# A hybrid DeltaNet and sparse-attention trunk on one core: the masks of the block inverse applied to its products, and background steps offered every 128 channels

## The chip, the core and the metric

The kernel runs on one core of one Trainium2 chip. The core has a matrix engine (TensorE, in the profile PE, its weight loads PEld) and three others that work on rows of elements: VectorE (DVE), ScalarE (ACT) and GpSimd (POOL). SyncE (SP) starts the loads of the weights. The engines run side by side, each through its own instructions in order, and wait for each other by semaphores. The metric is the time of one execution on the device, in microseconds (us).

## The reference, cut to what matters

One layer of gated DeltaNet, one of sparse attention, each followed by an MLP with squared ReLU, all with residual sums and RMS norms, for 256 tokens of width 2048. The part that the change touches is the DeltaNet layer's triangular system, for 32 value heads and chunks of 64 tokens:

```python
qkv, z, b, a = jnp.split(h @ w_in, [s1, s2, s3], axis=-1)
qkv = jax.nn.silu(_causal_conv(qkv, conv_w))        # four taps
l_mat = jnp.where(strict, jnp.einsum("nbhid,nbhjd->nbhij", kb, k) * decay, 0.0)
t_mat = lax.linalg.triangular_solve(eye + l_mat, eye, left_side=True, lower=True, unit_diagonal=True)
u = t_mat @ vb
w = t_mat @ (kb * jnp.exp(gc)[..., None])
...
o = rms_norm(o, out_norm) * jax.nn.silu(z)
```

## The kernel before, in words

All heavy products are of float32 numbers, each split into a high and a low part (the high part, whi, is a cast by ACT, the low part, wlo, a subtraction by DVE), and each product is three matmuls of such parts (`mm3`). The weights pass once: SP loads them in tiles of 1024 columns, and `Stream.get` (L144) splits the tile three places ahead before the matmuls of the present one are issued. So each weight tile brings one cast of 128x1024 on ACT and one subtraction of 128x1024 on DVE, always on time or TensorE waits.

Two helpers run over the weight tiles. `by_channel` (L359) takes two slices of 128 rows (k) per tile, and for each slice four blocks of 128 channels; a block is three matmuls of 256 columns, a slice 12, a tile 24. `by_token` (L377) has the tokens as the stationary side, and its matmuls are 512 columns wide, or 256 in the z projection.

Everything else in the program is background work: generators (`decays`, `delta`, `solved`, `transposed`, the attention's `attend` and others) that issue a piece, yield, and are resumed at a tick. `Background.tick` (L122) resumes a generator once its estimated time has come: the planner `Pace` (L36 to L70) keeps a clock for each engine by a formula of costs, and a step is due when the end of its chain plus 0.4 us is not after TensorE's clock. `yield True` also counts in the end of the last GpSimd operation. `ensure(key)` forces steps until an operand is there. So the order of the instructions on every engine is written at build time by this planner. In `by_channel` the tick stands behind each slice, that is after 12 matmuls.

The DeltaNet stage has 16 groups of two heads, each with eight weight tiles for q, k and v in `by_channel` and four for z in `by_token`. Behind the z tiles the group's two gates are made (zg: ACT's tanh, then a DVE product, twice). `delta` does the convolution (for each of four channels one ACT scaling and three DVE taps, y<-s,cw,y), the decays E (GpSimd), the products pk of keys and queries, and the factors la. Every second group, `solved` (L598) inverts the triangular factors of a pair of groups (eight pairs). It first copies the 32x32 diagonal blocks of la into Lc (16 small ACT copies), makes the inverse of the 2x2 diagonal blocks (Tct by two DVE operations, Tc by a transpose), and then goes through four levels (block sizes 2, 4, 8, 16). At each level: a product of 32 small matmuls in 32x32 tiles with a masked copy of Lc, a copy of it out of PSUM to Pm, a second product with Tct, a subtraction from Tc, a transpose to Tct. The four masked copies (Lm) are made by one GpSimd product of 128x1024 in the space of yv, which is why the profile calls them yv. Pm is Lc's own space, so the copies to Pm read Lc<-aux in the profile. Then come the 64-row and 128-row steps, the solutions, and four transposes of the output (aux<-wide,Tt) per chunk of heads, which the out-projection reads as h.

At the start of each MLP the residual sums of the last 512 columns (h<-acc,h on DVE, `chunk_done`) are transposed by a background generator (pk<-wide,h or aux<-wide,h), while `by_channel` has begun on the earlier columns. The engines' operations all pass through a helper, so every row of the profile says L81.

Of the kernel before, what the change touches and what calls it, by code (L numbers as in the profile page):

```python
# [11 lines left out]
OP = mybir.AluOpType  # L12
AX = mybir.AxisListType

P = 128
# [4 lines left out]
B = 32  # L20
LEVELS = (2, 4, 8, 16)
# [155 lines left out]
def tile_hybrid_trunk(ctx: ExitStack, tc: tile.TileContext, a: dict, out: bass.AP):  # L177
# [3 lines left out]
    act, dve, pool, pe = (pace.engine(n, e) for n, e in (("act", nc.scalar), ("dve", nc.vector), ("pool", nc.gpsimd), ("pe", nc.tensor)))  # L181
# [12 lines left out]
    bg = Background(pace)  # L194
    ws = Stream(pace, sync, act, dve, rawp, partp, 4, 4)

    def acc():
        return accp.tile([P, 512], F32, name="acc")
# [3 lines left out]
    def aux():  # L202
        if spare:
            spare.append(spare.pop(0))
            if spare[0]:
                return pkp.tile([P, 512], F32, name=spare[0])
        return auxp.tile([P, 512], F32, name="aux")
# [78 lines left out]
    fine = const.tile([P, 2 + len(LEVELS), B], F32, name="fine")  # L286
# [34 lines left out]
    def mm3(o, stat, mov, start, stop):  # L321
        (sh, sl), (mh, ml) = stat, mov
        pe.matmul(o, lhsT=sh, rhs=mh, start=start, stop=False, skip_group_check=True)
        pe.matmul(o, lhsT=sh, rhs=ml, start=False, stop=False, skip_group_check=True)
        pe.matmul(o, lhsT=sl, rhs=mh, start=False, stop=stop, skip_group_check=True)
# [19 lines left out]
    def ensure(key):  # L345
        while key not in ready:
            assert bg.step(), key
# [11 lines left out]
    def by_channel(n_items, part, key, n_ct=4, ahead=0):  # L359

        banks = [acc() for _ in range((n_ct + 1) // 2)]
        k0 = 0
        for _ in range(n_items):
            hi, lo = ws.get()
            n = hi.shape[1]
            for j in range(n):
                k = k0 + j
                ensure((key, min(k + ahead, n_items * n - 1)))
                for ct in range(n_ct):
                    s = slice(ct * P, ct * P + P)  # L370
                    mm3(banks[ct // 2][:, (ct % 2) * T:(ct % 2) * T + T], (hi[:, j, s], lo[:, j, s]), part(k),
                        k == 0 and ct % 2 == 0, False)
                bg.tick()
            k0 += n
        return banks

# [25 lines left out]
    with tc.tile_pool(name="first", bufs=1) as fp:  # L402
        xin = fp.tile([P, 2, D], F32, name="xin")
        rows = fp.tile([P, P], F32, name="rows")
# [8 lines left out]
        for name, src in (  # L413
# [3 lines left out]
            n = src.shape[0] // P  # L417
# [49 lines left out]
        bg.step()  # L467
        bg.step()
        first_banks = by_channel(8, x_part, "x0", ahead=3)
        bg.drain()  # L470

# [4 lines left out]
    with tc.tile_pool(name="delta", bufs=2, reuse_waits="tile") as dp:  # L476
# [43 lines left out]
        def delta(g, s, zg):  # L520
# [74 lines left out]
            if j == 1:  # L595
                yield from solved(p, *zip(*pairs[p]))

        def solved(p, la, r, rs, zg):  # L598

            H, U = range(4), [(i, b) for i in range(4) for b in range(2)]  # L600
            n_u = len(U)
            while p and ("o", 4 * p - 1) not in ready:
                yield
            rows = lambda q, n=1: slice(B * q, B * (q + n))
            flat = lambda x: x.rearrange("p u c -> p (u c)")
            one = lambda shape, name: dp.tile([P] + shape, F32, name=name, bufs=1)
            Lc, Tc, Tct = (one([n_u, B], n) for n in ("Lc", "Tc", "Tct"))
            Tt, yv = one([4, 2, P], "Tt"), one([4, 2, P], "yv")
            Pm, fold = Lc, yv.rearrange("p i b c -> p (i b c)")
            Lm = fold.rearrange("p (n u c) -> p n u c", n=len(LEVELS), u=n_u)  # L610
            pool.memset(Tt, 0.0)
            for j in range(2):
                for b in range(2):
                    for q in range(4):
# [3 lines left out]
            each = lambda x: x.unsqueeze(1).to_broadcast([P, n_u, B])  # L618
            n_l = len(LEVELS)
            dve.tensor_tensor(Tct, Lc, each(fine[:, 1]), op=OP.mult)  # L620
            dve.tensor_tensor(Tct, Tct, each(fine[:, 0]), op=OP.add)
            dve.transpose(flat(Tc), flat(Tct))
            pool.tensor_tensor(Lm, Lc.unsqueeze(1).to_broadcast([P, n_l, n_u, B]),
                               fine[:, 2:].unsqueeze(2).to_broadcast([P, n_l, n_u, B]), op=OP.mult)
            yield True
            small_bank = lambda w=B: aux()[:, 0:n_u * w].rearrange("p (u c) -> p u c", u=n_u)
            for n in range(n_l):
                t = small_bank()
                for u in range(n_u):
                    for q in range(4):  # L630
                        pe.matmul(t[rows(q), u], lhsT=Lm[rows(q), n, u], rhs=Tc[rows(q), u], start=True, stop=True)
                act.copy(Pm, t)
                yield
                t = small_bank()
                for u in range(n_u):
                    for q in range(4):
                        pe.matmul(t[rows(q), u], lhsT=Tct[rows(q), u], rhs=Pm[rows(q), u], start=True, stop=True)
                dve.tensor_tensor(Tc, Tc, t, op=OP.subtract)
                dve.transpose(flat(Tct), flat(Tc))
                yield  # L640
# [3 lines left out]
            t = small_bank()  # L644
# [11 lines left out]
            t = small_bank()  # L656
# [8 lines left out]
            t = small_bank(2 * B)  # L665
# [4 lines left out]
            t = small_bank(2 * B)  # L670
# [15 lines left out]
            t = aux()  # L686
# [10 lines left out]
            for j in range(2):  # L697
                t = aux().rearrange("p (i b d) -> p i b d", i=2, b=2)
# [27 lines left out]
            for j in range(2):  # L726
                t = aux()
# [8 lines left out]
        for g in range(DN_G):  # L736
            banks = first_banks if g == 0 else by_channel(8, x_part, "x0")
            if g > 1:
                ensure(("v", g - 2))
            s = dp.tile([P, 4, T], F32, name="s")  # L740
            for c in range(2):
                act.copy(s[:, 2 * c:2 * c + 2].rearrange("p n t -> p (n t)"), banks[c])
            if g == 0:
                bg.add(decays(by_channel(2, x_part, "x0", n_ct=1)[0]))
            zo = by_token(4, x_part, "x0", n_cols=256)
            if g > 4:
                ensure(("o", 2 * g - 9))
            zg = dp.tile([P, 2, T], F32, name="zg", bufs=5)
            for b in range(2):
                act.activation(zg[:, b], zo[b], AF.Tanh, scale=0.5)  # L750
                dve.scalar_tensor_tensor(zg[:, b], zg[:, b], 1.0, zo[b], op0=OP.add, op1=OP.mult)
            bg.add(delta(g, s, zg))
# [80 lines left out]
    with tc.tile_pool(name="dsa", bufs=1, reuse_waits="tile") as sp, ExitStack() as late:  # L833
# [165 lines left out]
        for c in range(4):  # L999
# [8 lines left out]
            for j in range(0, 4, 2):  # L1008
                if 4 * c + j >= 8:
                    ensure(("qa", 4 * c + j - 7))  # L1010
                t = acc()
                for i in range(2):
                    for k in range(2):
                        s = slice(k * P, k * P + P)
# [21 lines left out]
    for c in range(2):  # L1036
        s = slice(c * 1024, c * 1024 + 1024)
# [14 lines left out]
def _consts():  # L1052
    import numpy as np

    i, j = np.arange(P)[:, None], np.arange(P)[None, :]
    c = [np.eye(P), j >= i]
    i, j = i % B, j[:, :B]
    c += [i == j, -((i % 2 == 0) & (j == i + 1)).astype(np.float32)]
    for s in LEVELS:
        c.append((i // (2 * s) == j // (2 * s)) & (j % (2 * s) >= s) & (i % (2 * s) < s))  # L1060
    return np.concatenate([np.asarray(x, np.float32) for x in c], axis=1)


# [16 lines left out]
```

## Time and profile before

| what | value |
|---|---|
| median of 3 runs | 2609.01 us (2606.13 to 2609.33) |
| profiled execution | 2608.86 us |
| its span | 2607.1 us |
| mean granted clock of TensorE | 0.997 |
| TensorE (PE) busy | 98% of the span |
| DVE, ACT, POOL busy | 59%, 49%, 12% |

The span runs from the first to the last recorded instruction; the execution's own time has 1.8 us around it. A matmul's row gives its start and a modelled end: matmuls are pipelined, so the next one starts well before the row's end, and the time that a wait costs is best read from start to start. In the rows below "idle before" is the time in which the engine did nothing before the row, and the name behind the arrow is what it waited for. The DeltaNet stage lies between 135 and 790 us, the first MLP begins near 936 us.

### The profile page before, as it was taken

How to read it: one execution, taken by the hardware profiler on the slowest of the kernel's cores; microseconds unless marked ns; L12 is line 12 of the kernel's file. 1: busy time of each engine (PE TensorE's matmuls, PEld its weight loads, DVE VectorE, ACT ScalarE, POOL GpSimd, SP SyncE). 2: the span in 40 equal slices, each digit the busy share in tenths (PEclk: the TensorE clock that was granted, in tenths of full speed). 3: DMA queues.
4: the chain of work that ended last, by engine and by line, in shares of the span. 5: the costliest groups of instructions: out<-in, count | busy, mean ns of one | idle time of the engine just before them, and what ended most of it. 6: DMA issues, size and time to landing. Idle time of an engine off the chain costs nothing.

```text
span 2607.1 us, 52386 instructions
## 1 busy us (share of the span) xinstructions
PE 2559.3 (98%) x21795; PEld 2345.4 (90%) x21795; DVE 1534.1 (59%) x2164; ACT 1272.6 (49%) x1888; POOL 304.0 (12%) x514
## 2 busy tenths in 40 slices
PE   7999999999999999999999999999999999999997
PEld 7999999999978799988899988898899988999886
DVE  5867677768764555554455554676555544455544
ACT  5555555555554444443344444566444433444443
POOL 0434344434331000000000000000000000000000
PEclk9999999999999999999999999999999999999999
DMA  6655555555544566666666666644666666666664
GB/s 192 189 146 158 140 147 156 146 155 150 153 166 142 175 190 194 194 192 193 193 187 186 191 188 188 180 140 134 181 191 194 194 194 193 188 186 187 192 194 137
DMA packets 325389, 455.90 MB, mean 175 GB/s; under 512 B 18280, under 2 KB 159840, under 8 KB 324768
## 3 DMA queue, kind: packets, MB, share of 16 engines
q1 hardware_dynamic: 321888, 443.85, 56.9%
q10 hardware_dynamic: 2928, 7.37, 0.9%
q8 instruction: 170, 2.79, 0.4%
q0 software_dynamic: 336, 1.34, 0.2%
q14 instruction: 67, 0.55, 0.1%
HBM read 450.37 MB, written 2.13 MB: 174 GB/s over the span
## 4 chain that ended last, share of the span: by engine, by line
PE 90%; DVE 5%; ACT 2%; issue 1%; DMA 1%; POOL 0%; SPq 0%; ACTq 0%; DVEq 0%; POOLq 0%
PE acc L81 81%; PE aux L81 6%; PE pk L81 3%; DVE wlo L81 2%; ACT Lc L81 1%; DVE Tct L81 1%; DMA raw<-in_dn_w_in 1%; DVE y L81 1%; ACT whi L81 1%; DMA xin<-in_x 0%; DVE Tc L81 0%; ACT acc L81 0%; DVE p L81 0%; DVE h L81 0%; DVE Tt L81 0%
## 5 line engine op out<-in xcount | busy, mean ns | idle before, releaser
L81 DVE TENSOR_TENSOR wlo<-raw,whi 128x1024 fp32r<-128x1024 f32 x838 | 1027.2, 1233 | 869.7 <-ACT whi L81 860.4
L81 ACT CAST whi<-raw 128x1024 fp32r<-128x1024 f32 x838 | 874.1, 1048 | 865.4 <-PE acc L81 816.5
L81 PE MATMUL acc<-xhi,whi 128*128 128x256 f32 x3088 | 871.0, 282 | 0.3 <-ACT whi L81 0.3
L81 PE MATMUL acc<-xhi,wlo 128*128 128x256 f32 x3088 | 860.8, 279 | 1.2 <-DVE wlo L81 1.2
L81 PE MATMUL acc<-xlo,whi 128*128 128x256 f32 x3088 | 860.8, 279 | 0.0
L81 PE MATMUL acc<-whi,h 128*128 128x512 f32 x2688 | 847.2, 392 | 4.0 <-ACT acc L81 2.0
L81 PEld LDWEIGHTS acc<-whi,h 128*128 128x128 f32 x2688 | 504.8, 188 | 111.5 <-ACT acc L81 2.9
L81 PEld LDWEIGHTS acc<-xhi,wlo 128*128 128x128 f32 x3088 | 585.2, 190 | 1.7 <-DVE wlo L81 1.7
L81 PEld LDWEIGHTS acc<-xhi,whi 128*128 128x128 f32 x3088 | 581.4, 188 | 2.8 <-ACT whi L81 0.7
L81 PEld LDWEIGHTS acc<-xlo,whi 128*128 128x128 f32 x3088 | 581.8, 188 | 0.2
L81 PE MATMUL acc<-wlo,h 128*128 128x512 f32 x1344 | 524.6, 390 | 0.0
L81 PEld LDWEIGHTS acc<-wlo,h 128*128 128x128 f32 x1344 | 252.7, 188 | 50.1
L81 PE MATMUL acc<-whi,xhi 128*128 128x256 f32 (+2 forms) x576 | 171.4, 298 | 0.0
L81 PE MATMUL acc<-whi,xlo 128*128 128x256 f32 (+2 forms) x576 | 166.2, 288 | 0.0
L81 PE MATMUL acc<-wlo,xhi 128*128 128x256 f32 (+2 forms) x576 | 166.1, 288 | 0.0
L81 POOL TENSOR_SCALAR E<-R,tokc 128x128 f32<-128x128 f32 x96 | 104.5, 1103 | 144.9 <-DMA raw<-in_dn_w_in 81.2
L81 POOL DMA_DIRECT2D gain<-in_norm_final x1 | 0.7, 652 | 957.4 <-DVE nm L81 957.4
L81 PEld LDWEIGHTS acc<-whi,xhi 128*128 128x128 f32 x576 | 108.1, 188 | 2.6
L81 PEld LDWEIGHTS acc<-whi,xlo 128*128 128x128 f32 x576 | 108.2, 188 | 1.3
L81 PEld LDWEIGHTS acc<-wlo,xhi 128*128 128x128 f32 x576 | 108.1, 188 | 1.3
L81 DVE SCALAR_TENSOR_TENSOR y<-s,cw,y 128x255 f32<-128x255 f32 (+2 forms) x192 | 93.4, 487 | 13.3 <-ACT y L81 8.6
L81 POOL TENSOR_TENSOR h<-h,gain 128x512 f32<-128x512 f32 x8 | 10.1, 1282 | 777.4 <-ACT acc L81 777.4
(249 smaller groups left out, 1940.7 us busy)
## 6 DMA issues: line engine op xcount, KB each, us to landing
raw<-in_mlp_w_up SPq DMA_DIRECT2D x256, 512.0 KB, 4.3
raw<-in_mlp_w_down SPq DMA_DIRECT2D x256, 512.0 KB, 4.2
raw<-in_dn_w_in SPq DMA_DIRECT2D x66, 512.0 KB, 4.3
raw<-in_dn_w_in SPq DMA_DIRECT2D x256, 128.0 KB, 2.6
raw<-in_dn_w_in SPq DMA_DIRECT2D x128, 256.0 KB, 3.3
raw<-in_dn_w_out SPq DMA_DIRECT2D x64, 512.0 KB, 3.7
raw<-in_dsa_w_out SPq DMA_DIRECT2D x32, 512.0 KB, 4.0
raw<-in_dsa_w_uq SPq DMA_DIRECT2D x16, 512.0 KB, 4.3
```

Of the source, the lines that this page charges most:

```text
L81: r = f(*args, **kwargs)
```

## The change

`by_channel` calls the tick behind each block of 128 channels (3 matmuls) and no longer behind each slice (12 matmuls). In `solved` the four masked copies and their GpSimd product are gone: the first product of a level takes Lc as it is, and DVE multiplies the product by the mask of the level on its way out of PSUM into a tile Pm of its own, where ACT had copied it. The masks in the constants are transposed for that. The step behind the transpose to Tc yields without waiting for GpSimd.

```diff
--- before.py
+++ after.py
@@ -370,7 +370,7 @@
                     s = slice(ct * P, ct * P + P)
                     mm3(banks[ct // 2][:, (ct % 2) * T:(ct % 2) * T + T], (hi[:, j, s], lo[:, j, s]), part(k),
                         k == 0 and ct % 2 == 0, False)
-                bg.tick()
+                    bg.tick()
             k0 += n
         return banks
 
@@ -604,10 +604,9 @@
             rows = lambda q, n=1: slice(B * q, B * (q + n))
             flat = lambda x: x.rearrange("p u c -> p (u c)")
             one = lambda shape, name: dp.tile([P] + shape, F32, name=name, bufs=1)
-            Lc, Tc, Tct = (one([n_u, B], n) for n in ("Lc", "Tc", "Tct"))
+            Lc, Tc, Tct, Pm = (one([n_u, B], n) for n in ("Lc", "Tc", "Tct", "Pm"))
             Tt, yv = one([4, 2, P], "Tt"), one([4, 2, P], "yv")
-            Pm, fold = Lc, yv.rearrange("p i b c -> p (i b c)")
-            Lm = fold.rearrange("p (n u c) -> p n u c", n=len(LEVELS), u=n_u)
+            fold = yv.rearrange("p i b c -> p (i b c)")
             pool.memset(Tt, 0.0)
             for j in range(2):
                 for b in range(2):
@@ -620,16 +619,15 @@
             dve.tensor_tensor(Tct, Lc, each(fine[:, 1]), op=OP.mult)
             dve.tensor_tensor(Tct, Tct, each(fine[:, 0]), op=OP.add)
             dve.transpose(flat(Tc), flat(Tct))
-            pool.tensor_tensor(Lm, Lc.unsqueeze(1).to_broadcast([P, n_l, n_u, B]),
-                               fine[:, 2:].unsqueeze(2).to_broadcast([P, n_l, n_u, B]), op=OP.mult)
-            yield True
+            yield
             small_bank = lambda w=B: aux()[:, 0:n_u * w].rearrange("p (u c) -> p u c", u=n_u)
             for n in range(n_l):
                 t = small_bank()
                 for u in range(n_u):
                     for q in range(4):
-                        pe.matmul(t[rows(q), u], lhsT=Lm[rows(q), n, u], rhs=Tc[rows(q), u], start=True, stop=True)
-                act.copy(Pm, t)
+                        pe.matmul(t[rows(q), u], lhsT=Lc[rows(q), u], rhs=Tc[rows(q), u], start=True, stop=True)
+
+                dve.tensor_tensor(Pm, t, each(fine[:, 2 + n]), op=OP.mult)
                 yield
                 t = small_bank()
                 for u in range(n_u):
@@ -1057,7 +1055,7 @@
     i, j = i % B, j[:, :B]
     c += [i == j, -((i % 2 == 0) & (j == i + 1)).astype(np.float32)]
     for s in LEVELS:
-        c.append((i // (2 * s) == j // (2 * s)) & (j % (2 * s) >= s) & (i % (2 * s) < s))
+        c.append((i // (2 * s) == j // (2 * s)) & (i % (2 * s) >= s) & (j % (2 * s) < s))
     return np.concatenate([np.asarray(x, np.float32) for x in c], axis=1)
```

The order of the instructions changes on every engine. The first place is DVE in the sixth pair's solve: Tct and Tc are the 2x2 inverse, zg the gates of the group, y<-s,cw,y the convolution taps, wlo the low parts of the weights. Before:

```order
L81 TENSOR_TENSOR Tct<-Lc,fine 128x256
L81 TENSOR_TENSOR Tct<-Tct,fine 128x256
L81 STREAM_TRANSPOSE Tc<-Tct 128x256
L81 SCALAR_TENSOR_TENSOR y<-s,cw,y 128x255
L81 SCALAR_TENSOR_TENSOR y<-s,cw,y 128x254
L81 SCALAR_TENSOR_TENSOR y<-s,cw,y 128x253
L81 TENSOR_TENSOR wlo<-raw,whi 128x1024 x2
L81 SCALAR_TENSOR_TENSOR y<-s,cw,y 128x255
L81 SCALAR_TENSOR_TENSOR y<-s,cw,y 128x254
L81 SCALAR_TENSOR_TENSOR y<-s,cw,y 128x253
L81 TENSOR_TENSOR wlo<-raw,whi 128x1024
L81 TENSOR_TENSOR Tc<-Tc,aux 128x256
```

After, at the same place, up to the first mask product (Pm):

```order
L81 TENSOR_TENSOR Tct<-Lc,fine 128x256
L81 TENSOR_TENSOR Tct<-Tct,fine 128x256
L81 STREAM_TRANSPOSE Tc<-Tct 128x256
L81 SCALAR_TENSOR_TENSOR zg<-zg,acc 128x256 x2
L81 TENSOR_TENSOR wlo<-raw,whi 128x1024 x2
L81 SCALAR_TENSOR_TENSOR y<-s,cw,y 128x255
L81 SCALAR_TENSOR_TENSOR y<-s,cw,y 128x254
L81 SCALAR_TENSOR_TENSOR y<-s,cw,y 128x253
L81 TENSOR_TENSOR Pm<-aux,fine 128x256
```

The two zg gates and one more wlo now stand between Tc and the first DVE operation that follows a product, which is the mask product and no longer the subtraction from Tc.

The second place is TensorE at the start of the first MLP: acc<-whi,h and acc<-wlo,h are the last matmuls of the out-projection, the 256-wide rows are the MLP's first products, and pk<-wide,h are the first transposes of the last residual sums. Before, from the second of the MLP's matmuls on:

```order
L81 MATMUL acc<-xlo,whi 128x256
L81 MATMUL acc<-xhi,wlo 128x256
L81 MATMUL acc<-xhi,whi 128x256
L81 MATMUL acc<-xlo,whi 128x256
L81 MATMUL acc<-xhi,wlo 128x256
L81 MATMUL acc<-xhi,whi 128x256
L81 MATMUL acc<-xlo,whi 128x256
L81 MATMUL acc<-xhi,wlo 128x256
L81 MATMUL acc<-xhi,whi 128x256
L81 MATMUL acc<-xlo,whi 128x256
L81 MATMUL acc<-xhi,wlo 128x256
L81 MATMUL pk_12933<-wide,h 128x128 x2
```

After:

```order
L81 MATMUL acc<-wlo,h 128x512
L81 MATMUL acc<-whi,h 128x512
L81 MATMUL acc<-xhi,whi 128x256
L81 MATMUL acc<-xlo,whi 128x256
L81 MATMUL acc<-xhi,wlo 128x256
L81 MATMUL pk_12924<-wide,h 128x128 x2
```

The transposes stood behind 12 matmuls of the MLP and now stand behind 3. The second MLP begins in the same way.

## Rows read from the trace of the kernel before

**Rows 1.** Windows: stretch, us, busy per engine (instructions), granted clock, DMA share, GB/s
```profile
135.00:740.00 605.00, 595.40 (x8696) 570.20 (x8696) 432.74 (x797) 341.01 (x655) 240.39 (x405) 1.00 0.54 152
740.00:790.00 50.00, 47.77 (x286) 38.31 (x285) 28.46 (x53) 25.60 (x56) 14.43 (x30) 0.97 0.38 126
```

**Rows 2.** TensorE's waits, 135 to 740 us: who waited for whom, total us, times, longest
```profile
PE aux L81 <- DVE Tc L81: 6.5, 10, 1.6
PE aux L81 <- ACT Lc L81: 1.8, 1, 1.8
```

**Rows 3.** Timeline of the sixth pair: start us, us, engine, operation [idle before, releaser]
```profile
597.39 0.84 ACT L81 ACTIVATE r<-aux,nk 128x256 f32<-128x256 f32 x2 [0.87 <-PE aux L81]
...
598.64 1.06 ACT L81 CAST whi<-raw 128x1024 fp32r<-128x1024 f32 x1
...
599.60 4.05 ACT L81 COPY Lc<-la 32x64 f32<-32x64 f32 x16
...
603.69 0.42 DVE L81 TENSOR_TENSOR Tct<-Lc,fine 128x256 f32<-128x256 f32 x1 [1.03 <-ACT Lc L81]
...
603.74 2.66 POOL L81 TENSOR_TENSOR yv<-Lc,fine 128x1024 f32<-128x1024 f32 x1 [4.62 <-ACT Lc L81]
...
604.15 2.53 DVE L81 TENSOR_TENSOR Tct<-Tct,fine 128x256 f32<-128x256 f32 x1
...
606.36 5.08 POOL L81 TENSOR_SCALAR E<-R,tokc 128x128 f32<-128x128 f32 x4
...
606.71 0.45 DVE L81 STREAM_TRANSPOSE Tc<-Tct 128x256 f32<-128x256 f32 x1
...
607.08 1.48 DVE L81 SCALAR_TENSOR_TENSOR y<-s,cw,y 128x255 f32<-128x255 f32 x3
...
607.30 0.74 PE L81 MATMUL aux<-Tc,yv 32*32 32x32 f32 x64 [0.47 <-DVE Tc L81]
...
608.48 2.45 DVE L81 TENSOR_TENSOR wlo<-raw,whi 128x1024 fp32r<-128x1024 f32 x2
```

**Rows 4.** Timeline of ACT and DVE, 583 to 589 us, two gates
```profile
586.98 0.41 DVE L81 SCALAR_TENSOR_TENSOR zg<-zg,acc 128x256 f32<-128x256 f32 x1
...
587.43 0.38 ACT L81 ACTIVATE zg<-acc 128x256 f32<-128x256 f32 x1 [2.33 <-DVE zg L81]
```

**Rows 5.** Timeline of DVE, 612 to 618 us
```profile
613.45 0.41 DVE L81 TENSOR_TENSOR Tc<-Tc,aux 128x256 f32<-128x256 f32 x1
...
616.22 2.75 DVE L81 TENSOR_TENSOR wlo<-raw,whi 128x1024 fp32r<-128x1024 f32 x2 [0.78 <-ACT whi L81]
```

**Rows 6.** Timeline of PE, sixth pair: 24 matmul steps, then a small product
```profile
603.84 0.28 PE L81 MATMUL acc<-xhi,wlo 128*128 128x256 f32 x1
...
606.56 0.28 PE L81 MATMUL acc<-xhi,wlo 128*128 128x256 f32 x1
...
618.83 0.28 PE L81 MATMUL acc<-whi,xlo 128*128 128x256 f32 x1
619.03 0.75 PE L81 MATMUL aux<-Lc,Tct 32*32 32x32 f32 x64
619.72 0.39 PE L81 MATMUL acc<-whi,xhi 128*128 128x256 f32 x1
```

**Rows 7.** Timeline of PE, tail of the stage, 762.8 to 771.5 us
```profile
762.87 0.39 PE L81 MATMUL acc<-whi,h 128*128 128x512 f32 x1
...
767.03 1.22 PE L81 MATMUL acc<-whi,h 128*128 128x512 f32 x2 [1.01 <-DVE h L81]
...
771.05 0.64 PE L81 MATMUL aux<-wide,Tt 128*128 128x128 f32 x4
```

**Rows 8.** Timeline of DVE and PE, start of the first MLP
```profile
936.06 1.28 DVE L81 TENSOR_TENSOR h<-acc,h 128x512 f32<-128x512 f32 x2
...
936.39 0.28 PE L81 MATMUL acc<-xhi,whi 128*128 128x256 f32 x1
...
937.80 0.38 PE L81 MATMUL pk<-wide,h 128*128 128x128 f32 x2
```

## The prediction

> **What bounds the kernel now.** I read first the busy time by stage, then who TensorE waits for, then the timeline of one pair. In the DeltaNet stage (135 to 740 us) TensorE is busy for 595.4 of 605.0 us at the full granted clock, and the other engines for 72% or less [rows 1]: the kernel is bound by TensorE's own instructions, and only what makes it wait can be won. Its waits there are few and short, and nearly all stand before the small products of the triangular inverse: ten on Tc for 6.5 us and one on ACT's copy for 1.8 us [rows 2]. The reader is to see that all of it is 9.6 us of 2607, so the change can move the time by some tenths of a per cent either way.
>
> The sixth pair shows how such a wait comes about [rows 3]. ACT makes 16 copies to Lc in 4.05 us. DVE then makes Tct in 0.42 us, but its second, equal instruction takes 2.53 us, because it started while GpSimd made the four masked copies (2.66 us). Then 0.45 us for the transpose, and TensorE, idle for 0.47 us, starts. From the last main matmul (606.56) to the first small one (607.30) are 0.74 us, where an undisturbed entry takes 0.20 (618.83 to 619.03) [rows 3, 6]: 0.54 us lost. So a wait costs about 0.07 us more than its idle time; over a dozen waits 9.6 becomes 10.4 us.
>
> By the Trainium skill, "SBUF — State Buffer", section "Who interferes with whom", a DVE instruction with two SBUF inputs contends with a GpSimd instruction that reads SBUF, and one with at most one SBUF input doesn't. The 2.53 against 0.42 us agrees, but two wlo of DVE (two SBUF inputs each) take 2.45 us, 1.22 each, under GpSimd's E operations (5.08 us) [rows 3], which it would not let one expect. By it alone the mask products, whose one input is in PSUM, never wait for GpSimd, and the sum would lose 2.1 us of DVE time a pair.
>
> **The change, part by part.** *Removed:* GpSimd's product, 8 x 2.66 us, and ACT's 32 copies of 128x256, 0.38 us each by the like form [rows 3, 4]. Neither engine is what ends the stage, so the instructions themselves are worth nothing. What counts is DVE's hold, 2.53 - 0.42 = 2.1 us a pair. *Added:* 32 mask products on DVE, priced as the subtraction of the same shape out of PSUM, 0.41 us [rows 5]: 13 us of DVE that lie beside TensorE, except where TensorE waits for them. *Moved:* the planner now looks for a due step every 3 matmuls (0.34 us) and no longer every 12 (1.36 us), and waits for no GpSimd end. So it places the first product earlier, by about the 2 us that the hold had cost. What is won on DVE is given back by the place.
>
> Steady pair, counted from the start of the 24 matmuls during which ACT comes to Lc. ACT: it is free about 0.5 us after the tile starts, and its cast and two scalings of r, 0.96 + 0.84 us in before [rows 3], end at 2.3; 16 copies end at 6.3; DVE's 0.42 + 0.42 + 0.45 us with gaps give Tc at 7.7. TensorE by the new order: 24 matmuls (2.72 us [rows 6]), four transposes (0.4), 24 more, then 9: 2.72 + 0.45 + 2.72 + 9 x 0.113 + 0.09 = 7.0. It waits 0.7 us.
> Second product: DVE has two zg gates behind Tc, in turn with ACT (0.41 and 0.38 us, each waiting for the other [rows 4]), so ACT's next cast starts only at 8.4 and ends at 9.4. Then come two wlo (to 11.8), three convolution taps (1.48, to 13.3) and the mask product at 13.65. TensorE: product 0.69 and 0.12 on its return [rows 6], 36 matmuls, entry: 7.75 + 0.81 + 4.08 + 0.09 = 12.7. It waits 0.95 us. The new wait is one for a mask product that stands behind wlo and taps in DVE's queue, and behind it stand the next wlo.
> The third product comes with its operand (0.05); the fourth waits 0.4: 18 matmuls and a product are 2.9 us, DVE needs 3.35 for subtraction, transpose, taps and mask product. Sum 2.1 us a pair. The bounds of a pair: 0, if every queue has caught up, and 3.3, if the fifth to eighth products wait like the fourth.
>
> The sum, against the profiled execution:
> - Seven pairs in 135 to 740 us: 10.4 us before; after 2 x 1.8 (the first two have no earlier pair beside them) + 5 x 2.1 = 14.1: +3.7.
> - Eighth pair, which is solved after 740 us: no wait before; its first product now stands one tile behind the copies: +1.1 (0 to 2.1).
> - The transposes of the decays, three steps of the planner earlier: +0.3.
> - The tail of the stage. TensorE runs from 762.87 to 771.05 us, 8.2 us, for seven wide matmuls (0.23 each), four transposes (0.4) and the pk group (2.15): 4.0 us are lost [rows 7]. The granted clock of these 50 us is 0.97 [rows 1], 1.5 us at full speed, of which I count 0.5 on top. The sixth pair's transposes, which stood here a few matmuls ahead of their use, now come 30 wide matmuls (6.9 us) earlier. So I take the waits and with them the fall of the clock as gone: -4.5 (bounds: -2.2, the idle time alone, and -5.5).
> - The start of each MLP. The residual sums that the first transposes read end at about 937.3 (936.06 + 1.28), and 12 matmuls (936.39 to 937.80) cover them [rows 8]. The new order puts the transposes behind 3: TensorE comes at 936.8. It waits 0.6 us, twice: +1.2.
> - Attention: at about a dozen places a step moves up by 3 to 9 matmuls (0.35 to 1.0 us); one wait of 1.1 us goes, two or three come: +1.0 (-1.5 to +2.5).
> - More interruptions of the main stream: by the order of the two kernels 256 in place of 242. One costs the entry (0.09 over a matmul's step) and the return (0.12), if nothing joins it with a neighbour: 14 x 0.2 = 2.8 at most, 0 at least; most are transposes of the main stream's own shape: +0.5.
>
> 3.7 + 1.1 + 0.3 - 4.5 + 1.2 + 1.0 + 0.5 = +3.3; 2608.86 + 3.3 = **2612.2 us**. The profiled execution lies 0.15 us under the median of before, and I make nothing of that.
>
> On the interruptions the 32x32 products show 0.09 us on the way in and 0.12 on the way back [rows 6]. By the Trainium skill, "TensorEngine Tiling (Array Packing)", section "Tiling Modes", a change of tiling mode drains TensorE and a change of tile doesn't: by it the 32x32 products pay and the steps of 128 cost nothing. No run here shows the second; the sum by it would keep between 0 and 2.8 us here.
>
> **Rivals.**
> *A, the hold was the whole cause (faster).* DVE has Tc 2.1 us earlier, and the waits on Tc go. For it: ten of the waits in the stage are on Tc [rows 2], and each steady pair has the 2.53 us instruction. It decides if DVE has caught up with wlo and taps by the time of each product, which the account above denies by less than 1 us a product. Price: -10.4 for the pairs, -4.5 for the tail, +3.0 for the rest: 2608.9 - 11.9 = 2597 us.
> *B, DVE's queue runs later than I count (slower).* GpSimd's E operations hold DVE's wlo: two took 2.75 us at 616.22, 0.3 more than the two at 608.48 [rows 3, 5]. As each product now needs DVE twice in its chain, before and after, what is late there is late for TensorE; before, ACT freed the product. It decides where the waits exceed about 2.6 us a pair; with 3.3 us in all pairs but the first it is 7 x 1.2 = 8 us above the forecast: 2620 us. Against it: with the masked copies gone GpSimd is done earlier in each pair. If TensorE's waits then draw the granted clock down at one place, as at 0.97 in [rows 1], that is 1.5 us more.
> *C, the tail keeps its waits.* They hang on the last pair's chain through ACT and DVE, and the new place of the sixth pair's transposes is no help if the seventh's is late. Then the sum is +7.8: 2616.7 us.
>
> **How the numbers follow.** Forecast 0.50, A 0.16, B 0.22, C 0.12. The forecast's own range, from the bounds of its terms, is 2606 to 2617. The range reaches half way to A and to B: 2600 to 2620. About 0.2%, 5.2 us, is what a measurement of this kernel can tell from no change, so faster is under 2603.8 and slower over 2614.2. Faster: A with 0.15 and a hundredth of the forecast. Slower: B 0.19, C 0.08, forecast 0.06. The rest, 0.51, lies within.
>
> **What would show it.** In the changed profile DVE's two Tct take 0.42 us each; TensorE's waits in 135 to 740 us come to some 14 us, the larger part on Pm (mask product) and no longer on Tc. Around 763 to 772 us there is neither a wait over 0.3 us nor a lower granted clock. At the start of each MLP two waits of about 0.6 us stand before pk<-wide,h. Waits on Tc and Pm under 4 us in all would show A; over 20 us B; a lower granted clock in the slice at 765 us C. A wrong step would most likely be the place of DVE's queue: an error of 1 us there is 7 us in the sum.

## The result, and the profile after

The changed kernel takes 2622.61 us (median of 4 runs, 2620.49 to 2624.35) against 2608.06 us for the kernel before in the same comparison: ratio 1.0054, interval 1.0042 to 1.0065. It is 14.5 us slower; 3.3 us were forecast, and the time lies 2.6 us above the range.

By stage (stretch, us, busy time of PE, PEld, DVE, ACT and POOL, granted clock, DMA share, GB/s), after:

```profile
76.00:82.00 6.00, 4.87 (x28) 4.87 (x29) 3.86 (x8) 2.94 (x5) 0.00 (x0) 0.72 0.52 131
135.00:740.00 605.00, 586.02 (x8638) 561.36 (x8638) 414.56 (x806) 326.53 (x615) 218.05 (x392) 1.00 0.52 145
740.00:790.00 50.00, 48.82 (x240) 40.02 (x238) 34.73 (x67) 29.60 (x63) 20.55 (x36) 1.00 0.58 196
```

In the DeltaNet stage TensorE now idles for 19.0 us of the same 605, where it idled for 9.6 [rows 1]. The tail (740 to 790) has 1.2 us of idle time at a granted clock of 1.00, and had 2.2 us at 0.97. A new stretch of low clock stands at 76 to 82 us (0.72). TensorE's waits in the stage, in the columns of [rows 2]:

```profile
PE aux L81 <- DVE Pm L81: 7.2, 11, 1.1
PE aux L81 <- DVE Tc L81: 5.5, 7, 1.3
PE aux L81 <- DVE h L81: 3.8, 5, 0.8
```

To the waits on Tc, nearly as long as before, come 7.2 us on the mask product Pm and 3.8 us on h, the emptying of the PSUM bank of the output transposes. The sixth pair, which answers to [rows 3], on ACT and DVE:

```profile
597.28 4.23 ACT L81 COPY Lc<-la 32x64 f32<-32x64 f32 x16
...
601.54 0.43 DVE L81 TENSOR_TENSOR Tct<-Lc,fine 128x256 f32<-128x256 f32 x1 [3.88 <-ACT Lc L81]
...
602.00 0.42 DVE L81 TENSOR_TENSOR Tct<-Tct,fine 128x256 f32<-128x256 f32 x1
...
602.46 0.45 DVE L81 STREAM_TRANSPOSE Tc<-Tct 128x256 f32<-128x256 f32 x1
...
602.83 0.38 DVE L81 SCALAR_TENSOR_TENSOR zg<-zg,acc 128x256 f32<-128x256 f32 x1
...
603.65 2.00 ACT L81 CAST whi<-raw 128x1024 fp32r<-128x1024 f32 x2
...
603.66 0.42 DVE L81 SCALAR_TENSOR_TENSOR zg<-zg,acc 128x256 f32<-128x256 f32 x1 [0.45 <-ACT zg L81]
...
604.73 2.36 DVE L81 TENSOR_TENSOR wlo<-raw,whi 128x1024 fp32r<-128x1024 f32 x2 [0.65 <-ACT whi L81]
...
607.01 1.60 DVE L81 SCALAR_TENSOR_TENSOR y<-s,cw,y 128x255 f32<-128x255 f32 x3
...
608.54 0.41 DVE L81 TENSOR_TENSOR Pm<-aux,fine 128x256 f32<-128x256 f32 x1
```

and on TensorE:

```profile
603.05 0.74 PE L81 MATMUL aux<-Tc,Lc 32*32 32x32 f32 x64 [0.66 <-DVE Tc L81]
...
609.00 0.75 PE L81 MATMUL aux<-Pm,Tct 32*32 32x32 f32 x64 [0.91 <-DVE Pm L81]
```

DVE's second Tct takes 0.42 us where it took 2.53. By the Trainium skill, "SBUF — State Buffer", section "Who interferes with whom", that is what has to come of it once GpSimd no longer reads SBUF beside it, and the trace agrees. But the first product still waits (0.66 us of idle time), the 16 copies of ACT (4.23 us) having ended at 601.5. Behind Tc stand the two gates, two wlo and three taps, and only then, at 608.54, the mask product: TensorE idles 0.91 us more. The waits table also has pauses for which the profile names no releaser ("issue"): 2.1 us after in the stage, none before.

Both kernels have the same 15,744 matmuls in the main stream, in the same order, so that their starts can be compared one by one. The table has the start in before, and in the profiled runs of the others the difference to it, each counted from the start of its own span; a background step taken earlier also shows as a plus, so only rows 5100 and later count as lost or won time.

```
matmul  before us   after  masks only  ticks only  copies mended  6 matmuls + copies
   600       98.8    +0.6        -0.1        +0.3           -1.2                -0.9
  2400      372.7    +9.2        -3.0        +6.3           -1.6                -6.1
  3900      599.9   +16.7        -1.0       +16.7           -0.8                -7.0
  4500      692.2   +19.5        -1.8       +25.0           -0.2                -7.2
  5100      857.4   +11.6        +7.0       +17.0           -4.5                -9.0
  5700      968.7   +12.1        +7.0       +17.6           -4.0                -8.9
 11400     1919.1   +15.5        +7.0       +21.2           -0.5                -9.0
```

So of the 15.5 us of the changed kernel's profiled run 11.6 arise up to the end of the DeltaNet layer's out-projection, 0.6 at each MLP's start and 2.8 in the attention.

### The profile page after: what moved, and what is told of

Same layout as the page of the kernel before. It is cut to its first block, busy times and chain, and to the rows that moved or that the text cites. A ratio compares the mean times of both kernels' runs of the same rounds, so it can differ in the third digit from the quotient of the medians.

```text
span 2622.6 us, 52359 instructions
## 1 busy us (share of the span) xinstructions
PE 2562.6 (98%) x21795; PEld 2347.2 (89%) x21795; DVE 1528.8 (58%) x2196; ACT 1265.8 (48%) x1856; POOL 289.2 (11%) x506
## 4 chain that ended last, share of the span: by engine, by line
PE 90%; DVE 5%; ACT 2%; DMA 1%; issue 1%; ACTq 0%; SPq 0%; DVEq 0%
PE acc L81 82%; PE aux L81 6%; PE pk L81 3%; DVE wlo L81 2%; ACT Lc L81 1%; DVE y L81 1%; ACT whi L81 1%; DVE Tt L81 0%; DMA raw<-in_dn_w_in 0%; DVE h L81 0%; DMA xin<-in_x 0%; DVE Tct L81 0%; DMA R<-gl_dram 0%; DVE Tc L81 0%; DVE Pm L81 0%
## 5 line engine op out<-in xcount | busy, mean ns | idle before, releaser
L81 POOL TENSOR_SCALAR E<-R,tokc 128x128 f32<-128x128 f32 x96 | 92.5, 978 | 277.8 <-DMA R<-gl_dram 124.6
```

The costliest lines, as they stand in the source:

```text
L81: r = f(*args, **kwargs)
```

## The experiments

Two theories were set against each other. Theory 1, the place: the planner's clocks run ahead of the chip, a tick every 3 matmuls lets it issue steps that much too early, and the coarse tick had rounded the error away. Theory 2, the load: DVE with 32 more products in its queue is what is late, wherever the steps stand. All ratios are to the kernel before.

**Masks alone** (the tick back behind 12 matmuls):

```diff
-                    bg.tick()
+                bg.tick()
```

> The changed masks, the old tick (every 12 matmuls). Theory 1 (the place: with a tick every 3 matmuls the planner, whose clocks run 1 to 2 us ahead of DVE and ACT, issues steps before their operands or PSUM banks are there; the coarse tick had rounded this away): within 4 us of before, 2604 to 2612, the transposes of the outputs (aux<-wide,Tt) without a wait, waits before Pm under 6 us in all. Theory 2 (the load: 32 mask products in DVE's queue behind wlo and taps): 2615 to 2620, waits before Pm as in the changed kernel, 7 us or more.

2615.93 us, ratio 1.0033 (1.0020 to 1.0046). Its stages (columns as above) and the wait that matters in the second one:

```profile
135.00:740.00 605.00, 596.74 (x8630) 570.14 (x8629) 425.27 (x824) 331.53 (x620) 214.91 (x397) 1.00 0.55 154
740.00:790.00 50.00, 40.77 (x263) 32.79 (x262) 22.57 (x50) 23.15 (x52) 10.85 (x32) 0.90 0.30 95
```

```profile
PE aux L81 <- DVE Tt L81: 7.5, 1, 7.5
```

The stage up to 740 us is no worse than before (8.3 us idle, 9.6 before), and at 757 us of before the main stream is 7.6 us ahead; at 765 us it is 7.7 behind. Nearly all of that is one wait of 7.5 us and the low clock (0.90) around it. It is a step forced by its deadline: the out-projection asks (`ensure`) for the outputs of the seventh pair, whose chain isn't done, and the steps are issued one behind the other with nothing between them. Counted while the program is built, `ensure` forces one such step of the DeltaNet layer in before, none in after, seven here. Theory 1 said within 4 us and theory 2 at least 7; the total is theory 2's, the place of the loss neither's.

**Ticks alone** (the old masks, the tick behind 3 matmuls):

```diff
-                bg.tick()
+                    bg.tick()
```

> The old masks (GpSimd's masked copies, ACT's copy to Pm), the new tick (every 3 matmuls). Theory 1 (place): most of the 14 us, 2615 to 2622: the transposes of the outputs wait 1 us a pair, the MLPs' starts 0.6 us each, the attention 2 to 3 us, the decays fall to the lower clock, and the solves wait 1 to 2 us a pair. Theory 2 (load): 2609 to 2613, only the waits outside the solves.

2630.70 us, 1.0088 (1.0074 to 1.0101), 22.5 us slower and more than either theory gave. Nearly all its waits in the stage and the tail, some 17 us, stand on Tc (130 to 870 us):

```profile
PE aux L81 <- DVE Tc L81: 17.2, 15, 2.3
```

There is no mask product on DVE here, so the fine tick alone brings a loss. Behind five of these waits the granted clock falls, behind an equally long one it doesn't (6 us around each, columns as above):

```profile
340.00:346.00 6.00, 4.50 (x153) 4.29 (x154) 5.76 (x10) 2.82 (x4) 0.70 (x2) 1.00 0.65 186
527.00:533.00 6.00, 5.44 (x148) 5.20 (x149) 4.32 (x10) 2.32 (x4) 1.42 (x2) 0.72 0.67 184
```

Each fall is worth about 1.7 us (6 us at 0.72, an estimate), the five together 8.4; the changed kernel has one. That may be most of the 8 us between the two kernels. That the masks save them by giving DVE back GpSimd's hold is not shown.

**A longer margin everywhere** (0.4 to 0.8 us):

```diff
-    SLACK = 0.4
+    SLACK = 0.8
```

> The changed kernel with the planner's margin after each step raised from 0.4 to 0.8 us. Theory 1 (place): each of the some 35 waits shrinks by up to 0.4 us and those of 0.4 go: 2608 to 2614. Theory 2 (load): DVE's queue is what is late, and the waits move with it: 2618 or more.

**Costs raised for all small operations:**

```diff
-            cost = 0.1 + n / 1200.0 + ...
+            cost = (0.2 if n <= 256 else 0.1) + n / 1200.0 + ...
-            cost = max(0.2, 0.065 + n * ... / 960.0)
+            cost = max(0.2, (0.16 if n <= 512 else 0.09) + n * ... / 960.0)
```

> The changed kernel with the planner's costs set nearer to the measured ones: ACT's small operations 0.1 us dearer (a copy of 64 elements 0.25 in place of 0.15), DVE's operations of up to 512 elements 0.095 us dearer (a tap 0.43 in place of 0.33), the larger ones 0.025. Theory 1 (place): the waits in the DeltaNet stage come to under 8 us, 2600 to 2608. Theory 2 (load): the order changes, the products still wait for DVE, 2614 or more.

2666.63 us, 1.0223 (1.0209 to 1.0237), and 2698.17 us, 1.0345 (1.0331 to 1.0360): both theories missed. In the first of them (135 to 860 us):

```profile
PE aux L81 <- DVE Tt L81: 22.5, 3, 7.7
```

Later steps lengthen each pair's chain beyond the two groups that it has, `ensure` forces dozens of steps, and each forced chain has waits of up to 7.7 us on Tt with a lower clock behind them. So the place has two prices: a step too early makes TensorE wait for its operand, a step too late runs into its deadline.

**A margin at the outputs alone, and one at the solves as well:**

```diff
                 if j == 0:
-                    yield
+                    yield 1.0
```
```diff
-            yield
+            yield 0.7
             small_bank = ...
...
-                yield
+                yield 0.3 if n == 0 else 0.4
```

(A number that a step yields is added to the margin. The second edit has the first one in it.)

> The changed kernel, the planner's margin 1.0 us longer at one place alone: between the first and the second four transposes of a pair's output. Theory 1 (place: the step is issued before DVE has emptied the PSUM bank that it writes): the wait of 0.98 us before the second transposes goes in six pairs, nothing else changes: 2616 to 2619. Theory 2 (DVE is what is late, a wait that goes comes again at the next step that needs DVE): 2621 to 2624.

> As e5, and 0.7 us longer before the first product of each solve, 0.3 before the second, 0.4 before the second product of the later levels. No step is forced by a deadline in this order. Theory 1 (place): the waits of 0.73, 0.98 and 0.42 us go as well, about 2 us in each of six or seven pairs: 2603 to 2609. Theory 2 (load): the waits move on to later products: 2615 or more.

2623.83 us, 1.0061 (1.0048 to 1.0073), and 2615.69 us, 1.0026 (1.0017 to 1.0036): theory 1 missed both times, the numbers are theory 2's. In the first of them, without the wait before the output transposes, the first product of the sixth pair comes to this:

```profile
595.57 0.84 ACT L81 ACTIVATE r<-aux,nk 128x256 f32<-128x256 f32 x2 [1.64 <-POOL nk L81]
...
596.29 4.23 ACT L81 COPY Lc<-la 32x64 f32<-32x64 f32 x16
...
600.55 0.42 DVE L81 TENSOR_TENSOR Tct<-Lc,fine 128x256 f32<-128x256 f32 x1 [5.08 <-ACT Lc L81]
...
602.06 0.74 PE L81 MATMUL aux<-Tc,Lc 32*32 32x32 f32 x64 [2.17 <-DVE Tc L81]
```

and in the second, with 0.7 us more margin before this product:

```profile
602.60 0.45 DVE L81 STREAM_TRANSPOSE Tc<-Tct 128x256 f32<-128x256 f32 x1
...
603.19 0.74 PE L81 MATMUL aux<-Tc,Lc 32*32 32x32 f32 x64 [1.70 <-ACT whi L81]
```

(The profile names ACT there, but the product starts 0.14 us behind Tc's end, as in the changed kernel.) In the first, ACT's scaling of r waits for GpSimd's nk, the 16 copies follow, and the first product idles for 2.17 us in place of 0.66. The granted clock also falls three times more than in the changed kernel (0.72 over 327 to 333, 419 to 425 and 511 to 517 us). The chain from the keys' product to Tc goes over DVE, GpSimd and ACT and takes its time whatever TensorE did meanwhile: the wait of 1 us before the transposes had been spent beside it. A wait taken away upstream of a chain that is late anyway comes back at its end. It wasn't DVE's load, though, that it waited for: DVE had idled for 5.08 us until the copies came.

**The fine tick in the DeltaNet layer alone, and in its last groups alone:**

```diff
-                    bg.tick()
+                    if ct == n_ct - 1 or (key == "x0"):
+                        bg.tick()
```
```diff
+                    if ct == n_ct - 1 or (g >= 11):
```

> The changed kernel with the tick behind every 3 matmuls in the DeltaNet layer alone, behind 12 elsewhere. The two traces put 0.6 us at each MLP's start and 2.8 us in the attention to the finer tick: 2617 to 2620. If these differences were not the tick's: 2622 to 2623.

> The changed masks; the tick behind 3 matmuls in the DeltaNet groups 11 to 15 alone, behind 12 elsewhere. With the masks alone the stage was 7 us ahead of before at 757 us and lost 15 in a step forced by its deadline; in this order none is forced. Theory 1 (place and deadline, the two prices of the tick): 2599 to 2606, faster than before. Theory 2 (load): the tail loses as much as before or more, 2610 to 2618.

2618.97 us, 1.0042 (1.0029 to 1.0056): as expected, some 4 us lie in the MLPs and the attention. 2607.80 us, 0.9998 (0.9989 to 1.0007), between the two ranges: the forced steps of the masks-alone kernel and their 8 us are gone, as theory 1 said, but the last groups take back what I had hoped to keep, in waits of 1.2 to 1.6 us before output transposes and first products; it is the same as before, not faster.

**The mask products taken off DVE, TensorE's order unchanged:**

```diff
-                dve.tensor_tensor(Pm, t, each(fine[:, 2 + n]), op=OP.mult)
+                act._engine.copy(Pm, t)
+                pace.note("dve", "tensor_tensor", (Pm,), {})
```

> The changed kernel with every instruction of TensorE in its place, but ACT copies the product to Pm without a mask, where DVE had multiplied it (left out: the masks, so the inverse is another). It takes the 32 products from DVE's queue and nothing else. Theory 1 (place): the waits before Pm (7.2 us) go in part, those before Tc, the transposes, the MLPs and the attention stay: 2614 to 2619. Theory 2 (load: DVE's queue is late because of the mask products): the waits before Tc go too, 2605 to 2611.

2616.62 us, 1.0033 (1.0020 to 1.0045), as theory 1 had it. The waits (130 to 870 us):

```profile
PE aux L81 <- DVE Tc L81: 10.2, 15, 1.3
PE aux L81 <- DVE h L81: 3.8, 5, 0.8
```

The 7.2 us on Pm are gone, those on Tc have grown from 6.9 in after to 10.2, and those on h are the same. So 6 of the 14.5 us go with the mask products' place in DVE's queue (net of the 32 copies that ACT has in exchange), and 8.5 us don't.

**One cost mended:** ACT's operations of up to 64 elements, in effect the 16 copies to Lc, which the planner counts as 16 x 0.153 = 2.45 us and which take 4.05 [rows 3]:

```diff
-            cost = 0.1 + n / 1200.0 + ...
+            cost = (0.2 if n <= 64 else 0.1) + n / 1200.0 + ...
```

> The changed kernel with one cost of the planner mended: ACT's operations of up to 64 elements, the 16 copies to Lc above all, 0.25 us as measured and not 0.15. No step is forced in this order, and in it the mask product stands ahead of the convolution taps in DVE's queue. Theory 1 (place): the waits before the first product and the first mask product, 0.7 and 1.0 us in each of seven pairs, go: 2608 to 2613. Theory 2 (load): 2618 or more, since DVE has the same work.

2605.76 us, 0.9989 (0.9980 to 0.9998): 16.9 us under the changed kernel, and more than theory 1 gave. The masks, the fine tick and DVE's work are all as in the changed kernel. The sixth pair, and the stage:

```profile
588.54 4.24 ACT L81 COPY Lc<-la 32x64 f32<-32x64 f32 x16
...
593.78 0.45 DVE L81 STREAM_TRANSPOSE Tc<-Tct 128x256 f32<-128x256 f32 x1
...
594.15 1.18 DVE L81 TENSOR_TENSOR wlo<-raw,whi 128x1024 fp32r<-128x1024 f32 x1
...
594.37 0.74 PE L81 MATMUL aux<-Tc,Lc 32*32 32x32 f32 x64 [0.23 <-ACT y L81]
...
598.95 0.42 DVE L81 TENSOR_TENSOR Pm<-aux,fine 128x256 f32<-128x256 f32 x1
```

```profile
135.00:740.00 605.00, 599.91 (x8706) 573.87 (x8705) 425.53 (x826) 331.97 (x624) 211.77 (x397) 1.00 0.54 151
```

The first product now idles for 0.23 us (the profile names ACT, but it starts 0.14 us behind Tc's end, as before the mending), the mask product comes ahead of the taps behind the second and third wlo, the two gates stand ahead of Tc, and the idle time of the stage is 5.1 us, a quarter of the changed kernel's. Theory 2, that DVE's load makes it late wherever the steps stand, is refuted by this run: the load is the same and nearly all the loss is gone.

**A tick behind 6 matmuls in the DeltaNet layer, 12 elsewhere, alone and with the mended cost:**

```diff
-                    bg.tick()
+                    if ct == n_ct - 1 or (0 <= g and ct % 2):
+                        bg.tick()
```

> The changed masks, the tick behind 6 matmuls in the DeltaNet layer, behind 12 elsewhere. No step is forced. Theory 1 (place): between the ticks of 3 (2619 with them in this layer alone) and those of 12 without their forced step (about 2607): 2605 to 2613. Theory 2 (load): 2615 or more.

> e10 and e11 together: ticks behind 6 matmuls in the DeltaNet layer, 12 elsewhere, the cost of ACT's small copies mended. One step is forced, 0.4 us ahead of its planned time, as in before. Theory 1 (place): 2600 to 2608, the best of these. Theory 2 (load): 2613 or more.

2606.92 us, 0.9994 (0.9985 to 1.0003), in theory 1's range, and 2599.84 us, 0.9966 (0.9954 to 0.9978), just below it: 8.3 us under before, the best of all and faster than both kernels, with the changed masks. Its stages:

```profile
135.00:740.00 605.00, 603.36 (x8742) 577.18 (x8741) 429.89 (x830) 339.67 (x636) 212.72 (x400) 1.00 0.55 154
740.00:790.00 50.00, 47.80 (x451) 37.26 (x450) 28.41 (x57) 21.53 (x43) 10.28 (x28) 0.97 0.47 150
```

The stage idles for 1.6 us in place of 9.6. What is left stands in the tail, where it is as in before (2.2 us, clock 0.97).

## Why the prediction was wrong

The direction was right and the mechanism in part; the size was wrong by a factor of four. The step that failed is the sum over a pair: it followed the eight small products alone and put the output transposes, which the finer tick moves as well, at nothing in the stage. They lose 4.8 us. Step by step:

- *The steady pair, 2.1 us:* right. From start to start (the idle time of the rows and 0.07 more, as in the prediction) the sixth pair waits 0.73 before the first product, 0.98 before the second, 0.1 and 0.42 before the next two, 2.2 us together.
- *The first pairs at 1.8 to 2.1:* right too. Read the same way, the first four wait 1.8, 2.2, 2.1 and 2.1 us, and the products of all seven pairs together 14.7 us, where 14.1 were forecast. What comes on top in the second to fourth pair are pauses inside a product or the main stream, 2.9 us in all from start to start, for which the profile names no releaser:

```profile
344.77 0.72 PE L81 MATMUL aux<-Pm,Tct 32*32 32x32 f32 x61
346.55 0.25 PE L81 MATMUL aux<-Pm,Tct 32*32 32x32 f32 x3 [1.06 <-issue]
```

They are no waits for an operand that the profile shows. Before has none in the stage, the masks-alone kernel 1.0 us of idle time, the ticks-alone one none, that with the cost mended still 1.8; what they are stays open.
- *What the sum lacks, the step that failed:* the second four output transposes of a pair. I had followed them only in the tail. In the stage they moved from 12 to 6 matmuls behind the first four, and DVE, with two wlo ahead, hasn't emptied their PSUM bank:

```profile
585.94 2.34 DVE L81 TENSOR_TENSOR wlo<-raw,whi 128x1024 fp32r<-128x1024 f32 x2
...
587.96 0.28 PE L81 MATMUL acc<-whi,xlo 128*128 128x256 f32 x1
...
588.21 0.73 DVE L81 SCALAR_TENSOR_TENSOR h<-aux,vecs,h 128x512 fp32r<-128x512 f32 x1
...
589.00 0.66 PE L81 MATMUL aux<-wide,Tt 128*128 128x128 f32 x4 [0.76 <-DVE h L81]
```

0.76 us of idle time, 0.92 from start to start, in five pairs, and 0.3 in another (before: 0.6 in one). The experiment at the outputs shows that to remove it alone gains nothing, since the time is then lost before the first product.
- *The place as a fixed offset.* "What is won on DVE is given back by the place" was the right thought, but I took the place for an offset of about 2 us at the first product. Read from start to start over the seven pairs (the step to a product less its undisturbed 0.20 us, to a transpose less 0.12), the time lost is, in us:

```
run                  first products  later products  output transposes
before                          2.2             7.1                0.6
masks only                      6.5             1.6                0.1
ticks only                      6.0            13.7                1.4
after                           6.1             8.6                4.8
copies mended                   2.6             1.3                0.7
6 matmuls                       7.9             1.0                0.1
6 matmuls + copies              0.4             0.1                0.7
```

The planner's error on the 16 copies (1.6 us) stands before the first products: the coarse tick and GpSimd's end together had covered it in before, either alone doesn't, and with the cost mended it goes at both ticks. The finer tick costs most at the later products and the transposes. That these go too when the one cost is mended is what the runs show; the order behind the later first product is another, and which part of it does it was not tried.
- *The eighth pair, +1.1:* 1.4 before its first product, a pause of 0.4 in a later one, and 0.8 us before a product with r of the seventh pair that I hadn't counted.
- *The decays, +0.3:* the wait grew as forecast, from 1.49 us (first row, before) to 1.84 (second, after), but behind it the clock fell:

```profile
78.45 0.44 PE L81 MATMUL aux<-wide,E 128*128 128x128 f32 x2 [1.49 <-DVE E L81]
```
```profile
75.01 0.28 PE L81 MATMUL acc<-xhi,wlo 128*128 128x256 f32 x1
...
77.13 0.44 PE L81 MATMUL aux<-wide,E 128*128 128x128 f32 x2 [1.84 <-DVE E L81]
```

with 0.72 granted from 76 to 82 us, 1.7 us at full speed (an estimate).
- *The tail, -4.5:* right; the waits and the low clock are gone (740 to 790 above). By the count of [rows 3] the transposes that stood there are the seventh pair's, not the sixth's.
- *The MLPs' starts, +1.2:* right to a tenth. The second transpose comes at 948.96, after the residual sums:

```profile
947.62 1.28 DVE L81 TENSOR_TENSOR h<-acc,h 128x512 f32<-128x512 f32 x2
...
948.36 0.33 PE L81 MATMUL pk<-wide,h 128*128 128x128 f32 x1
...
948.96 0.33 PE L81 MATMUL pk<-wide,h 128*128 128x128 f32 x1 [0.27 <-DVE h L81]
```

- *The attention, +1.0 (-1.5 to +2.5):* 2.8, above the bound. Two waits in 1600 to 2000 us were not there before:

```profile
PE pk L81 <- DVE p L81: 1.2, 1, 1.2
PE acc L81 <- ACT h L81: 0.6, 1, 0.6
```

- *The interruptions, +0.5:* their price was not read apart; the traces have 14 more, as forecast.

Together: 0.6 us at the products, 4.8 at the transposes, 2.9 of pauses, 1.5 at the eighth pair, 1.7 of clock and 1.8 in the attention are 13.3 us above the sum; the profiled run lies 12.2 above it, so that readings of this kind close to about 1 us.

Of the rivals, B has the time (2620) but not the cause. Its mechanism was GpSimd's E operations on DVE's wlo; in the sixth pair these begin at 606.97, behind the two wlo of 604.73, and the wlo at 608.87 takes 1.24 us beside them, no more than one of those two (1.18). Nor do the pairs' products wait more than forecast. What it had right is the sentence that each product now needs DVE twice in its chain: that is the 6 us of the experiment without mask products. That its number is near the measured one is luck. A is refuted as a forecast, and yet the masks' gain exists: with them and the coarse tick the later products lose 1.6 us in place of 7.1, and with 6 matmuls and the cost mended the kernel is faster than before. Of C's tail nothing is seen.

What stays open: why the later products and the transposes come on time once the one cost is mended. Of the 16.9 us some 15 lie in the seven pairs by the table, 3.5 at the first products, 7.3 at the later ones and 4.1 at the transposes; the later first product and the changed order behind it (gates, wlo, taps) come from the one number and were not tried apart.

## What to carry to other kernels

Where a planner at build time sets the order, a finer grain brings its errors to light: before one makes ticks finer, compare its costs with the trace, the many small operations first. One such cost mended won 16.9 us here, but many costs raised at once lost 75.6 (2698.17 against 2622.61), so each has to be tried by itself. A wait ahead of a chain that is late anyway is not worth its length; ask what stands at the chain's end. And a margin for all steps is no cure, since a step that comes too late costs more, at its deadline, than one too early.

## What the hardware showed

The length of a wait alone did not decide the granted clock. Before the decays' transposes a wait of 1.49 us left it at full (before, 78.5 us), and one of 1.84 was followed by a stretch at the lower of the two levels in the changed kernel (77.1 us), but not in the kernel with the cost mended:

```profile
77.53 0.44 PE L81 MATMUL aux<-wide,E 128*128 128x128 f32 x2 [1.84 <-DVE E L81]
```
```profile
76.00:82.00 6.00, 4.47 (x39) 4.47 (x40) 3.89 (x8) 2.59 (x4) 0.00 (x0) 1.00 0.49 137
```

In [rows 3] two wlo took 2.45 us under GpSimd's four E operations, while a Tct took 2.53 in place of 0.42 under GpSimd's masked product: not every GpSimd operation that reads SBUF holds DVE. Beside such E operations the same Tct took 0.47 us (the run with both margins, 602.09 us).
